# A decoder block's first MLP stage: weight sums, operand parts and m5's subtractions moved between VectorE, ScalarE and GpSimd, and the gates' buffers regrouped

## The chip, the cores and the metric

The kernel runs on one core of a Trainium2 chip. The metric is the device time of one execution in microseconds. The core's engines are TensorE (PE in the rows; its weight loads are PEld), VectorE (DVE), ScalarE (ACT), GpSimd (POOL) and SyncE (SP, which only issues DMA transfers here). Each runs its own instructions strictly in order; semaphores tie them together.

## What is computed

A hybrid decoder block on 2048 tokens of width 1024. Cut to what matters here:

```python
y_attn = dilated_attention(q, k, v)              # width 256
y_gmlp = chunked_gmlp(u, z)                      # width 512
merged = gate_a * (y_attn @ w_branch_attn) + gate_b * (y_gmlp @ w_branch_gmlp)
x = x + rmsnorm(merged @ w_out)
h = rmsnorm(x)
a = relu(h @ w_mlp_in)                           # 1024 -> 4096: first MLP stage
x = x + rmsnorm((a * a) @ w_mlp_out)             # second MLP stage
```

`gate_a` and `gate_b` are sigmoids of columns of the block's first projection; they wait in DRAM (`gated`) until the merge.

## The kernel before

Every matrix product is made of three products of parts: an operand is split into a rounded high half (fp32r) and the rest, and high x high, high x low and low x high are added. A **split** is a ScalarE copy to the high half and a subtraction on VectorE or GpSimd for the low one. One product of 128 x 128 weights with 512 columns is one matmul in the rows.

**Merge** (about 1070 to 1400 us). Four chunks of 512 tokens, in the order 2, 3, 0, 1. `merge` runs over eight tiles `dt` of 128 channels. Each multiplies the attention branch (`b0`) and the gMLP branch (`b1`) on TensorE; VectorE multiplies each with its gate (L1211), adds the two (L1213), and the sum is split into `mg` (ScalarE L74, VectorE L82), from which `out_block` makes the output product `o`. A gate `g0_{c}{dt}` or `g1_{c}{dt}` is 256 KB, loaded by `load_gate` (SP L1185) into one of two pools' places and opened by ScalarE's sigmoid (L1194). A scheduler orders the instructions of this part from the order in which they are written and the places that are free. Between the gates run other transfers (`trw`, `tqw`, `spot`: sums of MLP weights and operands for the next stage).

**First MLP stage** (about 1406 to 1970 us). The 1024 x 4096 product is done as a two-level Strassen-like scheme: seven **outer products** o = 0 to 6, each with eight weight steps q (`hs_0` to `hs_55`, n = 8 o + q), each of seven small products i. That is 392 steps k, and in step k TensorE runs six matmuls or twelve in a row of two steps (L1572), into PSUM tiles `ha` (3 banks), `hb` and `hc` (3 banks together). Their results are read into the accumulators `X` (names `X`, `X_y`, `X_yt`, `X_xr`, `X_gpost`, `X_gmlp` for places in memory) or into a staging tile `e`: first reads on ScalarE (L1584) or VectorE (L1586), the others on VectorE (L1588). In this stage all engines run as written; `later(k, f, ...)` puts work behind step k.

- Weights: `hraw_n` is loaded (L1401), `combine` forms the seven parts: five sums of 256 columns on GpSimd (L1409 to L1415), and three splits `sa`, `sb`, `sc`. `staged` does such a split: ScalarE copies to the high half (L1350), copies the source once more to one of two PSUM banks (L1360), and VectorE subtracts from that (L1365).
- Operand parts: `hb` holds the raw operand of the next outer product (two at a time, `hb_o0` and `hb_o1`); its sums run on VectorE and GpSimd (`less_sub` L1469, `sum_hb` L1494). `ops_hb` splits part j into a place `spot`: if its engine is VectorE through `staged`, otherwise with one ScalarE copy (L1487) and GpSimd's subtraction (`later`'s line, L1984). At the seam of an outer product (q = 7) six parts j are split, two halves each.
- Late weight sums: `w_load`, `w_sum` and `w_store` prepare sums of `w_mlp_in` (tiles `wt`) for t = 11 to 15; `w_sum` has four operations (`which` 0 to 3), of which 0 (L1546) and 2 (L1550) are VectorE's, 1 (L1548) and 3 (L1552) GpSimd's, each waiting for the one before.
- m5: the fourth outer product's results are added to `X` and stored apart (`m5d`); after outer product 5's results have been stored they are loaded again and subtracted (`m5_sub`, L1609), four subtractions for each q, 32 in all.

Of the kernel before, what the change touches and what calls it, by code (L numbers as in the profile page):

```python
# [9 lines left out]
F32 = mybir.dt.float32  # L10
# [7 lines left out]
P = 128  # L18
# [24 lines left out]
def block_kernel(ctx, tc, a, out):  # L43
    nc = tc.nc
    pe, act, dve, pool, sp = nc.tensor, nc.scalar, nc.vector, nc.gpsimd, nc.sync
# [1005 lines left out]
    for n in range(len(units) + 1):  # L1051
        u = None
        if n < len(units):
            g, c, j = units[n]
# [85 lines left out]
    gtp = stack(e2b, "gtp", 2)  # L1140
# [39 lines left out]
    def load_gate(c, dt, wch):  # L1180
        if dt < KT and (c, dt, wch) not in gates:
            d = chunks.index(c) * KT + dt
            pl, tag = (gtp, f"gt{wch}") if c == 2 or d % (5 - 2 * wch) < 3 - wch else (gxp[0], f"gx{wch}")
            gt = pl.tile([P, 512], F32, name=f"g{wch}_{c}{dt}", tag=tag, bufs=3 - wch if pl is gtp else 2 - wch)
            sp.dma_start(gt, gate_d[wch * 8 + dt, :, c * 512:(c + 1) * 512])  # L1185
            gates[c, dt, wch] = gt

    opened, gxp, egx = set(), [], ExitStack()
# [8 lines left out]
    def merge(c, yt, between, each=None):  # L1197
        cs = slice(c * 512, (c + 1) * 512)
        mg = []
        for dt in range(KT):  # L1200
            dsl = slice(dt * P, (dt + 1) * P)
            if dt % 4 == 0:
                mg.append(mgp[dt // 4].tile([P, 2, 4, 512], F32R, name=f"mg{c}{dt}", tag="mg"))
            parts = []
            for wch, ks in ((0, range(0, 2)), (1, range(2, 6))):
                open_gate(c, dt, wch)
                gt = gates.pop((c, dt, wch))
                p = psum_mm(f"b{wch}_{c}{dt}")
                for k in ks:
                    mm3(p, wb[k][:, 0, dsl], wb[k][:, 1, dsl], yt[k][:, 0, :], yt[k][:, 1, :], k == ks[0], k == ks[-1])  # L1210
                dve.tensor_mul(gt, gt, p)  # L1211
                parts.append(gt)
            dve.tensor_add(parts[0], parts[0], parts[1])  # L1213
            split(mg[-1][:, 0, dt % 4, :], mg[-1][:, 1, dt % 4, :], parts[0])
            if c != 2:
                load_gate(c, dt + 5, 0)
                load_gate(c, dt + 3, 1)
            elif not dt:
                w = bot.tile([P, D], F32, name="gates3", tag="xr")
                for n, key in enumerate(((c, 5, 1), (c, 6, 0))):  # L1220
                    gates[key] = w[:, n * 512:(n + 1) * 512]
                    sp.dma_start(gates[key], gate_d[key[2] * 8 + key[1], :, c * 512:(c + 1) * 512])
            elif dt > 2:
                load_gate(c, dt + 3, 1)
                load_gate(c, dt + 4, 0)
            if dt < KT - 1:
                for wch in range(2):
                    open_gate(c, dt + 1, wch)
            if each:
                each(dt)  # L1230
            if dt in between:
                between[dt]()
        return mg
# [88 lines left out]
    W_EARLY = 11  # L1322
# [47 lines left out]
    NQ, HQ = NF // 2, NF // 4  # L1370
# [137 lines left out]
    def later(k, f, *args):  # L1508
        todo.setdefault(k, []).append((f, args))
# [32 lines left out]

    def w_sum(t, which):
        a11, a12, a21, a22 = outer_t["w", t]
        if which == 0:
            dve.tensor_add(a22, a21, a22)  # L1546
        elif which == 1:
            pool.tensor_sub(a21, a11, a21)  # L1548
        elif which == 2:
            dve.tensor_sub(a11, a22, a11)  # L1550
        else:
            pool.tensor_sub(a12, a12, a11)  # L1552

# [45 lines left out]
    m5_ = {}  # L1599
# [6 lines left out]
    def m5_sub(q, f):  # L1606
        for c in range(2):
            x_ = X[2 * q + f][:, c * 512:(c + 1) * 512]
            pool.tensor_sub(x_, x_, m5_.pop((q, f, c)))  # L1609

    def hstep(k, n, i):

# [21 lines left out]
                    later(k + ((7, 11, 16) if o + 1 in LESS else (3, 8, 16))[m] + w, sum_hb, key(o + 1, w), part, eng)  # L1634
        if q == HQ - 1 and USE[i][0] < 6:
            j = USE[i][0] + 1
            ops_hb(k, o + 1, j, (None if j == 1 else dve, dve if o in (0, 3) else pool))
            if j == 1:
                for w in range(2):
                    later(k + 3 + w, sum_hb, key(o + 1, w), "T4", (dve, pool)[w])  # L1640
# [31 lines left out]
    for n, c in enumerate(chunks):  # L1672
        if n:
            mg = merge(c, yt, {0: flush, 2: flush}, lambda dt: merge_pieces(c, dt))
        for i in range(4):
# [2 lines left out]
            last.append(b)  # L1678
            if n < 3 and not i:
                yt = load_y(chunks[n + 1])  # L1680
                for dt, wch in ((0, 0), (0, 1), (1, 0), (1, 1), (2, 0), (2, 1), (3, 0), (4, 0)):
                    with behind():
                        load_gate(chunks[n + 1], dt, wch)
            if n < 3:
# [262 lines left out]
        for f, d, args in ((outer_load, 0, ()), (outer_sum, 4, (0,)), (outer_sum, 6, (2,)), (outer_store, 9, ())):  # L1947
            later(t + d, f, n, *args)
    for n in range(NF // 2 - W_EARLY):
        t = (37, 43, 48, 124, 127)[n]  # L1950
        for f, d, args in ((w_load, 0, ()), (w_sum, 4, (0,)), (w_sum, 4, (1,)), (w_sum, 5, (2,)), (w_sum, 6, (3,)),
                           (w_store, 7, ())):
            later(t + d, f, W_EARLY + n, *args)
    for q in range(HQ):
        t = 7 * (5 * HQ + 4) + 19 * q // 2
        for f in range(2):
            later(t + 5 * f, m5_load, q, f)
            later(t + 5 * f + 5, m5_sub, q, f)
    gfin = None
    for k, (_, stage, n, i) in enumerate(yorder):  # L1960
        if not stage:
# [125 lines left out]
```

## Time and profile before

| what | value |
|---|---|
| time, median of 3 runs | 2595.82 us (2593.57 to 2597.63) |
| time of the profiled execution | 2597.95 us |
| its span, first to last instruction | 2596.2 us |
| mean granted clock of TensorE | 0.993 |
| TensorE / VectorE / ScalarE / GpSimd busy | 98% / 65% / 49% / 53% |

The rows further down are in microseconds from the start of the span. In a timeline a line has the start, the duration, the engine, the source line, the operation with its output and inputs, and in brackets the idle time of the engine just before, with what ended it. SPq is SyncE's queue. In a row of windows the granted clock of TensorE stands behind POOL: 1.00 is 2.4 GHz, 0.50 is 1.2 GHz.

### The profile page before, as it was taken

What the parts mean: (1) busy time and instruction counts of PE and PEld (TensorE: products, weight loads), DVE (VectorE), ACT (ScalarE), POOL (GpSimd) and SP (SyncE); (2) the same over time, 40 slices, a digit from 0 to 9 for tenths busy, and PEclk for the clock granted to TensorE, in tenths of its full rate; (3) what the DMA queues carried; (4) which work ended last, traced back from release to release, by engine and by line L of the source; (5) the groups of instructions that cost most, each with busy time, mean ns of one, the idle gap of its engine ahead of it and who ended that gap; (6) DMA issues with size and microseconds to landing.
All of it is one profiled execution on the core that took longest, in us unless ns stands there. A gap on an engine that the chain in (4) does not pass through costs nothing. (4 is left out here: it accounts for less than half of the span.)

```text
span 2596.2 us, 36297 instructions
## 1 busy us (share of the span) xinstructions
PE 2550.3 (98%) x12122; PEld 2126.4 (82%) x12122; DVE 1687.8 (65%) x3071; ACT 1282.7 (49%) x2702; POOL 1367.1 (53%) x1377
## 2 busy tenths in 40 slices
PE   9999999999999999999999999999999999999998
PEld 8888888888888887787787777878878888888886
DVE  5676565444443446776676678778877676666767
ACT  5213211244445434554435745675447676666755
POOL 0363254275545554311113757777798667777634
PEclk9999999999999999999999999999999999999999
DMA  8779778989897899877766766457884222122236
GB/s 319 281 248 327 256 233 277 316 251 287 269 325 228 228 291 327 283 253 249 266 235 234 244 202 211 139 175 214 265 269 146 84 95 72 67 90 90 90 114 211
DMA packets 413294, 568.73 MB, mean 219 GB/s; under 512 B 58930, under 2 KB 247602, under 8 KB 412083
## 3 DMA queue, kind: packets, MB, share of 16 engines
q1 hardware_dynamic: 387600, 504.73, 59.7%
q0 software_dynamic: 15616, 55.06, 5.5%
q10 hardware_dynamic: 9890, 6.62, 0.8%
q8 instruction: 96, 1.57, 0.2%
q14 instruction: 92, 0.75, 0.1%
HBM read 362.16 MB, written 204.14 MB: 218 GB/s over the span
## 5 line engine op out<-in xcount | busy, mean ns | idle before, releaser
L1572 PE MATMUL ha<-spot,hs 128*128 128x512 f32 x1344 | 327.9, 392 | 12.9 <-DVE e L1586 3.6
L1882 PE MATMUL ya<-spot,s 128*128 128x512 f32 x1344 | 324.0, 389 | 0.8 <-DVE X_yt L1890 0.5
L1572 PEld LDWEIGHTS ha<-spot,hs 128*128 128x128 f32 x1344 | 252.1, 188 | 69.9 <-DVE e L1586 5.2
L1882 PEld LDWEIGHTS ya<-spot,s 128*128 128x128 f32 x1344 | 252.0, 188 | 54.2 <-DVE X_yt L1890 0.9
L1350 ACT ACTIVATE s<-sraw 128x512 fp32r<-128x512 f32 x168 | 105.3, 627 | 152.5 <-POOL sraw L1411 113.3
L1350 ACT ACTIVATE hs<-hraw 128x512 fp32r<-128x512 f32 x168 | 105.1, 626 | 140.6 <-POOL hraw L1411 110.0
L1572 PE MATMUL hc<-spot,hs 128*128 128x512 f32 x672 | 173.4, 394 | 0.8 <-DVE X_y L1588 0.8
L731 PE MATMUL g<-opA,spots 128*128 128x512 f32 x672 | 171.4, 399 | 2.1 <-DVE cv L763 2.1
L1882 PE MATMUL yc<-spot,s 128*128 128x512 f32 x672 | 170.5, 389 | 0.0
L731 PE MATMUL g<-opB,spots 128*128 128x512 f32 x648 | 164.0, 397 | 0.0
L1572 PEld LDWEIGHTS hc<-spot,hs 128*128 128x128 f32 x672 | 128.2, 191 | 28.3 <-DVE X_y L1588 1.2
L99 PE MATMUL x<-hT_a,wq 128*128 128x512 f32 x384 | 149.7, 390 | 0.0
L100 PE MATMUL x<-hT_a,wq 128*128 128x512 f32 x384 | 149.4, 389 | 0.0
L101 PE MATMUL x<-hT_a,wq 128*128 128x512 f32 x384 | 149.4, 389 | 0.0
L1882 PEld LDWEIGHTS yc<-spot,s 128*128 128x128 f32 x672 | 126.1, 188 | 26.2
L74 ACT ACTIVATE hl<-r 128x512 fp32r<-128x512 f32 x48 | 30.4, 633 | 236.8 <-POOL r L332 89.0
L731 PEld LDWEIGHTS g<-opA,spots 128*128 128x128 f32 x672 | 121.5, 189 | 24.3 <-issue 2.5
L82 POOL TENSOR_TENSOR spots<-gr,spots 128x512 fp32r<-128x512 f32 x98 | 128.5, 1315 | 23.8 <-DMA gr<-in_w_in_dram 8.7
L1743 ACT ACTIVATE sraw<-sraw 128x1024 f32<-128x1024 f32 x128 | 134.7, 1052 | 1.7
L731 PEld LDWEIGHTS g<-opB,spots 128*128 128x128 f32 x648 | 116.9, 188 | 21.2
L82 POOL TENSOR_TENSOR spot<-w2r,spot 128x512 fp32r<-128x512 f32 x79 | 101.0, 1305 | 50.2 <-ACT spot L74 50.2
L76 POOL TENSOR_SCALAR spots<-gr 128x512 fp32r<-128x512 f32 x86 | 55.4, 644 | 130.6 <-PE g L731 92.6
(466 smaller groups left out, 6758.1 us busy)
## 6 DMA issues: line engine op xcount, KB each, us to landing
sraw<-sd SPq DMA_DIRECT2D x128, 256.0 KB, 3.3
qk<-hl SPq DMA_DIRECT2D x24, 1024.0 KB, 5.7
qq<-qk SPq DMA_DIRECT2D x96, 256.0 KB, 5.3
sd<-e SPq DMA_DIRECT2D x64, 256.0 KB, 4.6
hraw<-wsd SPq DMA_DIRECT2D x32, 512.0 KB, 4.7
w2r<-in_w_mlp_out_dram SPq DMA_DIRECT2D x16, 1024.0 KB, 9.0
g<-gated SPq DMA_DIRECT2D x56, 256.0 KB, 5.4
gr<-sgd SPq DMA_DIRECT2D x53, 256.0 KB, 4.9
```

What stands on the lines that cost most here:

```text
L74: act.activation(hi, src, AF.Copy)
L76: pool.tensor_scalar(hi, src, 1.0, 1.0, op0=OP.mult, op1=OP.mult)
L82: (pool if lo_eng == "pool" else dve).tensor_sub(lo, src, f32(hi))
L99: pe.matmul(ps, lh, rh, start=start, stop=False)
L100: pe.matmul(ps, lh, rl, start=False, stop=False)
L101: pe.matmul(ps, ll, rh, start=False, stop=stop)
L731: pe.matmul(p, w[:, l, k], h[:, r, k], start=i in (1, 6, 5, 4) and not k and not m, stop=k == 3 and m == 2, skip_group_check=True)
L1350: act.activation(hi, src, AF.Copy)
L1572: pe.matmul(p, w[:, l, S_AT[i], kk * P:(kk + 1) * P], b[r], start=i in (1, 2, 5) and not kk and not z, stop=kk == 1 and z == 2, skip_group ...
L1743: act.activation(sraw_[n], sraw_[n], func)
L1882: pe.matmul(p, s[:, l], w[r], start=i in (1, 2, 5) and not m and not o, stop=m == 1 and o == 2, skip_group_check=True)
```

## The change

Four things are changed.

1. `load_gate` spreads the gates over four places for each kind (before: five for `g0`, three for `g1`), and after tile `dt` loads both gates of `dt` + 4 (before: `g0` of `dt` + 5 and `g1` of `dt` + 3). Ahead of a chunk `g1` of tile 3 is loaded instead of `g0` of tile 4.
2. For t = 13, 14 and 15 all four operations of `w_sum` are GpSimd's. The loads of t = 14 and 15 go from steps 124 and 127 to 122 and 134, the sums and stores with them.
3. At the seams behind outer products 0 and 3, the second half of the parts j = 2, 4 and 6 is GpSimd's instead of VectorE's, which also drops the second ScalarE copy.
4. m5's loads and subtractions get other steps. The subtractions ran from step 313 on, every 9 or 10 steps for q (f = 1 five steps behind f = 0). Now they run at step 7 (40 + q) + 24 for q up to 3 (304 to 325) and + 38 from q = 4 on (346 to 367), f = 1 three steps behind f = 0, loads five steps ahead. For q over 3 the first of two subtractions is VectorE's (8 operations).

```diff
--- before.py
+++ after.py
@@ -1180,8 +1180,8 @@
     def load_gate(c, dt, wch):
         if dt < KT and (c, dt, wch) not in gates:
             d = chunks.index(c) * KT + dt
-            pl, tag = (gtp, f"gt{wch}") if c == 2 or d % (5 - 2 * wch) < 3 - wch else (gxp[0], f"gx{wch}")
-            gt = pl.tile([P, 512], F32, name=f"g{wch}_{c}{dt}", tag=tag, bufs=3 - wch if pl is gtp else 2 - wch)
+            pl, tag = (gtp, f"gt{wch}") if c == 2 or d % 4 < 3 - wch else (gxp[0], f"gx{wch}")
+            gt = pl.tile([P, 512], F32, name=f"g{wch}_{c}{dt}", tag=tag, bufs=3 - wch if pl is gtp else 1 + wch)
             sp.dma_start(gt, gate_d[wch * 8 + dt, :, c * 512:(c + 1) * 512])
             gates[c, dt, wch] = gt
 
@@ -1213,8 +1213,8 @@
             dve.tensor_add(parts[0], parts[0], parts[1])
             split(mg[-1][:, 0, dt % 4, :], mg[-1][:, 1, dt % 4, :], parts[0])
             if c != 2:
-                load_gate(c, dt + 5, 0)
-                load_gate(c, dt + 3, 1)
+                load_gate(c, dt + 4, 0)
+                load_gate(c, dt + 4, 1)
             elif not dt:
                 w = bot.tile([P, D], F32, name="gates3", tag="xr")
                 for n, key in enumerate(((c, 5, 1), (c, 6, 0))):
@@ -1542,12 +1542,13 @@
 
     def w_sum(t, which):
         a11, a12, a21, a22 = outer_t["w", t]
+        e = dve if t < W_EARLY + 2 else pool
         if which == 0:
-            dve.tensor_add(a22, a21, a22)
+            e.tensor_add(a22, a21, a22)
         elif which == 1:
             pool.tensor_sub(a21, a11, a21)
         elif which == 2:
-            dve.tensor_sub(a11, a22, a11)
+            e.tensor_sub(a11, a22, a11)
         else:
             pool.tensor_sub(a12, a12, a11)
 
@@ -1606,7 +1607,7 @@
     def m5_sub(q, f):
         for c in range(2):
             x_ = X[2 * q + f][:, c * 512:(c + 1) * 512]
-            pool.tensor_sub(x_, x_, m5_.pop((q, f, c)))
+            (dve if q > 3 and not c else pool).tensor_sub(x_, x_, m5_.pop((q, f, c)))
 
     def hstep(k, n, i):
 
@@ -1634,7 +1635,7 @@
                     later(k + ((7, 11, 16) if o + 1 in LESS else (3, 8, 16))[m] + w, sum_hb, key(o + 1, w), part, eng)
         if q == HQ - 1 and USE[i][0] < 6:
             j = USE[i][0] + 1
-            ops_hb(k, o + 1, j, (None if j == 1 else dve, dve if o in (0, 3) else pool))
+            ops_hb(k, o + 1, j, (None if j == 1 else dve, dve if o in (0, 3) and j % 2 else pool))
             if j == 1:
                 for w in range(2):
                     later(k + 3 + w, sum_hb, key(o + 1, w), "T4", (dve, pool)[w])
@@ -1678,7 +1679,7 @@
             last.append(b)
             if n < 3 and not i:
                 yt = load_y(chunks[n + 1])
-                for dt, wch in ((0, 0), (0, 1), (1, 0), (1, 1), (2, 0), (2, 1), (3, 0), (4, 0)):
+                for dt, wch in ((0, 0), (0, 1), (1, 0), (1, 1), (2, 0), (2, 1), (3, 0), (3, 1)):
                     with behind():
                         load_gate(chunks[n + 1], dt, wch)
             if n < 3:
@@ -1947,15 +1948,15 @@
         for f, d, args in ((outer_load, 0, ()), (outer_sum, 4, (0,)), (outer_sum, 6, (2,)), (outer_store, 9, ())):
             later(t + d, f, n, *args)
     for n in range(NF // 2 - W_EARLY):
-        t = (37, 43, 48, 124, 127)[n]
+        t = (37, 43, 48, 122, 134)[n]
         for f, d, args in ((w_load, 0, ()), (w_sum, 4, (0,)), (w_sum, 4, (1,)), (w_sum, 5, (2,)), (w_sum, 6, (3,)),
                            (w_store, 7, ())):
             later(t + d, f, W_EARLY + n, *args)
     for q in range(HQ):
-        t = 7 * (5 * HQ + 4) + 19 * q // 2
+        t = 7 * (5 * HQ + q) + (24 if q < 4 else 38)
         for f in range(2):
-            later(t + 5 * f, m5_load, q, f)
-            later(t + 5 * f + 5, m5_sub, q, f)
+            later(t + 3 * f - 5, m5_load, q, f)
+            later(t + 3 * f, m5_sub, q, f)
     gfin = None
     for k, (_, stage, n, i) in enumerate(yorder):
         if not stage:
```

From L1546 on a line of the new kernel has a number that is one higher. The first place is GpSimd's order in outer product 5, from the last sum of `hs_46` to the first of `hs_47`; `m5_...` are m5's tiles, `hb_61` the operand for outer product 6. Before:

```order
L1415 TENSOR_TENSOR hraw_46_16986<-hraw_46_16986 128x256
L1609 TENSOR_TENSOR X_yt4_13018<-X_yt4_13018,m5_000_17060 128x512
L1609 TENSOR_TENSOR X_yt4_13018<-X_yt4_13018,m5_001_17062 128x512
L1494 TENSOR_TENSOR hb_61_16810<-hb_61_16810 128x512
L1984 TENSOR_TENSOR spot0_12747<-hb_61_16810,spot0_12747 128x512
L1609 TENSOR_TENSOR X_yt5_13019<-X_yt5_13019,m5_010_17129 128x512
L1609 TENSOR_TENSOR X_yt5_13019<-X_yt5_13019,m5_011_17131 128x512
L1494 TENSOR_TENSOR hb_61_16810<-hb_61_16810 128x512
L1409 TENSOR_TENSOR hs_47_17193<-hraw_47_17075,hs_47_17193 128x256
```

and now:

```order
L1415 TENSOR_TENSOR hraw_46_16982<-hraw_46_16982 128x256
L1494 TENSOR_TENSOR hb_61_16798<-hb_61_16798 128x512
L1985 TENSOR_TENSOR spot0_12747<-hb_61_16798,spot0_12747 128x512
L1610 TENSOR_TENSOR X_yt1_13021<-X_yt1_13021,m5_110_17074 128x512
L1610 TENSOR_TENSOR X_yt1_13021<-X_yt1_13021,m5_111_17076 128x512
L1610 TENSOR_TENSOR X_yt2_13022<-X_yt2_13022,m5_200_17133 128x512
L1610 TENSOR_TENSOR X_yt2_13022<-X_yt2_13022,m5_201_17135 128x512
L1494 TENSOR_TENSOR hb_61_16798<-hb_61_16798 128x512
L1409 TENSOR_TENSOR hs_47_17199<-hraw_47_17079,hs_47_17199 128x256
```

The four subtractions in these rows are now those of `m5_110` to `m5_201`; the six of `m5_000` to `m5_101` stand ahead of `hs_46`.

The second place is VectorE's order in outer product 2, from a read of `hc_17` into `X_yt` to the read of `sb` for `hs_20`; `wt14x` and `wt15x` are tiles of the late weight sums. Before:

```order
L1588 TENSOR_TENSOR X_yt0_13020<-X_yt0_13020,hc_17_14705 128x512
L1546 TENSOR_TENSOR wt143_14716<-wt142_14715,wt143_14716 128x512
L1588 TENSOR_TENSOR X_0_13024<-X_0_13024,ha_19_14774 128x512
L1550 TENSOR_TENSOR wt140_14713<-wt143_14716,wt140_14713 128x512
L1588 TENSOR_TENSOR X_yt3_13023<-X_yt3_13023,ha_18_14676 128x512
L1365 TENSOR_TENSOR hs_20_14783<-sa_20_14786,hs_20_14783 128x512
L1588 TENSOR_TENSOR X_yt3_13023<-X_yt3_13023,hc_18_14802 128x512
L1546 TENSOR_TENSOR wt153_14754<-wt152_14753,wt153_14754 128x512
L1469 TENSOR_TENSOR hb_30_14573<-hb_30_14573 128x512
L1588 TENSOR_TENSOR X_0_13024<-X_0_13024,hb_19_14823 128x512
L1550 TENSOR_TENSOR wt150_14751<-wt153_14754,wt150_14751 128x512
L1365 TENSOR_TENSOR hs_20_14783<-sb_20_14821,hs_20_14783 128x512
```

and now:

```order
L1589 TENSOR_TENSOR X_yt0_13020<-X_yt0_13020,hc_17_14707 128x512
L1589 TENSOR_TENSOR X_0_13024<-X_0_13024,ha_19_14762 128x512
L1589 TENSOR_TENSOR X_yt3_13023<-X_yt3_13023,ha_18_14670 128x512
L1365 TENSOR_TENSOR hs_20_14774<-sa_20_14777,hs_20_14774 128x512
L1589 TENSOR_TENSOR X_yt3_13023<-X_yt3_13023,hc_18_14792 128x512
L1469 TENSOR_TENSOR hb_30_14567<-hb_30_14567 128x512
L1589 TENSOR_TENSOR X_0_13024<-X_0_13024,hb_19_14807 128x512
L1365 TENSOR_TENSOR hs_20_14774<-sb_20_14805,hs_20_14774 128x512
```

The four sums on `wt` tiles are gone; the reads of `ha`, `hb` and `hc` stand next to one another.

The third place is ScalarE's order in the merge of chunk 3: sigmoids of gates (L1194) and copies for the merged tile (`mg`, L74). Before:

```order
L1194 ACTIVATE g1_34_10931<-g1_34_10931 128x512
L74 ACTIVATE mg30_10856<-g0_32_10542 128x512
L1194 ACTIVATE g0_36_10929<-g0_36_10929 128x512
L1194 ACTIVATE g1_35_10966<-g1_35_10966 128x512
L74 ACTIVATE mg30_10856<-g0_33_10546 128x512
L1194 ACTIVATE g0_37_10964<-g0_37_10964 128x512
L1194 ACTIVATE g1_36_11009<-g1_36_11009 128x512
L74 ACTIVATE mg34_11019<-g0_34_10548 128x512
```

and now:

```order
L1194 ACTIVATE g1_35_10931<-g1_35_10931 128x512
L74 ACTIVATE mg30_10856<-g0_32_10542 128x512
L1194 ACTIVATE g0_35_10929<-g0_35_10929 128x512
L1194 ACTIVATE g1_36_10966<-g1_36_10966 128x512
L74 ACTIVATE mg30_10856<-g0_33_10546 128x512
L1194 ACTIVATE g0_36_10964<-g0_36_10964 128x512
L1194 ACTIVATE g1_37_11011<-g1_37_11011 128x512
L1194 ACTIVATE g0_37_11009<-g0_37_11009 128x512
L74 ACTIVATE mg34_11021<-g0_34_10884 128x512
```

`g0_35` and `g1_36` now have the places of `g0_36` and `g1_35`, and the sigmoid of `g0_37` stands ahead of the copy for `g0_34`.

## Rows read from the trace of the kernel before

**Rows 1.** The page's first part: engine, busy us (share of the span), instructions.

```profile
PE 2550.3 (98%) x12122; PEld 2126.4 (82%) x12122; DVE 1687.8 (65%) x3071; ACT 1282.7 (49%) x2702; POOL 1367.1 (53%) x1377
```

**Rows 2.** TensorE's waits, 1100 to 2000 us: us in total, times, longest.

```profile
PE b L99 <- DVE g L1211: 4.9, 3, 1.8
PE ha L1572 <- DVE e L1586: 3.6, 3, 2.2
PE ha L1572 <- DVE X_yt L1588: 2.5, 1, 2.5
PE ha L1572 <- DVE X L1588: 2.3, 1, 2.3
PE ha L1572 <- ACT X_y L1584: 1.5, 1, 1.5
PE ha L1572 <- ACT e L1584: 1.4, 1, 1.4
PE hc L1572 <- DVE X_y L1588: 0.8, 1, 0.8
```

**Rows 3.** Windows: us, busy us of PE, PEld, DVE, ACT, POOL; clock, DMA share, GB/s.

```profile
1267.10:1270.50 3.40, 3.40 (x9) 2.65 (x8) 3.37 (x7) 0.73 (x2) 0.72 (x1) 0.50 0.95 287
1499.20:1502.60 3.40, 3.40 (x9) 2.65 (x8) 3.16 (x6) 2.24 (x5) 1.94 (x3) 0.50 0.63 136
1608.40:1611.80 3.40, 3.40 (x10) 2.66 (x9) 3.40 (x5) 0.00 (x0) 3.24 (x4) 0.50 0.97 323
1891.70:1895.10 3.40, 3.40 (x8) 2.69 (x9) 3.40 (x6) 2.48 (x6) 3.40 (x4) 0.50 0.70 216
```

**Rows 4.** Timeline of ScalarE, chunk 3's merge: start, duration, [idle before <-releaser].

```profile
1179.67 0.63 ACT L1194 ACTIVATE g<-g 128x512 f32<-128x512 f32 x1 [4.34 <-DMA g<-gated]
```

**Rows 5.** Timelines of ScalarE and SyncE's queue at the end of chunk 1.

```profile
1357.14 0.63 ACT L74 ACTIVATE mg<-g 128x512 fp32r<-128x512 f32 x1 [2.08 <-DVE g L1213]
1355.42 0.33 SPq L1310 DMA_DIRECT2D tqw<-in_w_mlp_in_dram  x1
```

**Rows 6.** Timelines of ScalarE, VectorE and GpSimd, 1480 to 1501 us.

```profile
1485.48 0.60 ACT L1360 ACTIVATE sw<-hb 128x512 f32<-128x512 f32 x1 [0.26 <-DVE spot L1365]
1482.26 0.69 DVE L1550 TENSOR_TENSOR wt<-wt,wt 128x512 f32<-128x512 f32 x1 [0.70 <-POOL wt L1548]
1491.05 1.21 DVE L1550 TENSOR_TENSOR wt<-wt,wt 128x512 f32<-128x512 f32 x1 [0.81 <-POOL wt L1548]
1489.72 1.30 POOL L1548 TENSOR_TENSOR wt<-wt,wt 128x512 f32<-128x512 f32 x1 [3.72 <-DVE wt L1546]
1500.51 0.74 POOL L1409 TENSOR_TENSOR hs<-hraw,hs 128x256 fp32r<-128x256 f32 x1 [3.96 <-ACT hs L1407]
```

**Rows 7.** Timelines of VectorE and GpSimd, 1604 to 1607 us.

```profile
1604.10 1.75 DVE L1550 TENSOR_TENSOR wt<-wt,wt 128x512 f32<-128x512 f32 x1 [1.29 <-POOL wt L1548]
1606.38 0.67 DVE L1588 TENSOR_TENSOR X<-X,ha 128x512 f32<-128x512 f32 x1
1604.03 1.28 POOL L1469 TENSOR_TENSOR hb<-hb 128x512 f32<-128x512 f32 x1
```

**Rows 8.** Windows, the 20 us around outer product 4's first steps.

```profile
1720.00:1740.00 20.00, 17.26 (x74) 13.31 (x73) 16.91 (x29) 19.39 (x38) 13.54 (x14) 1.00 0.31 94
```

**Rows 9.** Windows at 1880 us; timelines of GpSimd, VectorE and ScalarE before it.

```profile
1880.00:1900.00 20.00, 17.52 (x71) 14.02 (x70) 12.21 (x21) 10.49 (x21) 19.37 (x20) 0.91 0.75 235
1841.36 1.30 POOL L1469 TENSOR_TENSOR hb<-hb 128x512 f32<-128x512 f32 x1 [4.85 <-DMA hb<-tqd]
1854.60 2.55 POOL L1609 TENSOR_TENSOR X_yt<-X_yt,m 128x512 f32<-128x512 f32 x2
1867.38 0.69 DVE L1365 TENSOR_TENSOR hs<-sb,hs 128x512 fp32r<-128x512 f32 x1 [1.99 <-ACT sb L1360]
1889.69 0.69 DVE L1365 TENSOR_TENSOR hs<-sb,hs 128x512 fp32r<-128x512 f32 x1 [5.15 <-ACT sb L1360]
1888.53 0.63 ACT L1350 ACTIVATE hs<-hraw 128x512 fp32r<-128x512 f32 x1 [4.31 <-POOL hraw L1411]
```

## The prediction

> **What bounds the kernel now.** I read the page's engine shares first, then TensorE's waits between 1100 and 2000 us (the merge and the first MLP stage, which hold everything that the diff touches), then its granted clock behind the gaps, then the timeline of each engine around them. TensorE is busy for 2550.3 of 2596.2 us [rows 1]: what can be won is a handful of short gaps, and no engine's average matters. The waits name them [rows 2]: three in the merge behind VectorE's gate product (4.9 us together), and in the first MLP stage 2.2 and 0.8 us at the seam of outer products 0 and 1 (and 1.5 behind ScalarE's `X_y`), 2.3 us in product 2, about 2.8 at the seam of 3 and 4 (ScalarE's 1.4, and the 1.4 that is left of VectorE's 3.6 without the 2.2), and 2.5 us in product 5. I call the last four A, B, C and D. Behind the longest of them, and behind one of the gates', the granted clock is 0.50 for 3.4 us (1.2 instead of 2.4 GHz) [rows 3], and 3.4 x 0.5 = 1.7 us of work is lost with it; behind the gaps of 1.5 us and less it is not. So 4.9 + 1.7 (gates), 2.2 + 0.8 + 1.7 (A without its 1.5), 2.3 + 1.7 (B), 2.8 (C) and 2.5 + 1.7 (D) are at stake, 22.3 us in all.
>
> **Gates: 0, from -6.6 to +1.** VectorE's gate product stands in its order behind the split of an earlier merged tile (`mg`), whose first half is ScalarE's; and ScalarE waits 4.34 us for a gate's transfer ahead of it [rows 4]. With the new places the second kind of gate is loaded for one tile step further ahead. But it goes out when it did: the place that `g1_35` took before, and `g1_36` takes now, comes free by a VectorE read of the same tile step, so the transfer leaves at the same instant and only its name is later. ScalarE's order shows the sigmoid of that transfer still in front of the split of `g0_33`: `g0_36, g1_35, split` became `g0_35, g1_36, split`. TensorE's next gate is there sooner, but the strict order keeps everything behind the one that lands last. So 0.
>
> At the end of chunk 1 the loads of two operands change places: `spot51` goes first, `spot41` behind one more 512 KB transfer, about where `tqw` went out at 1355.42 [rows 5]; and ScalarE and VectorE now split both ahead of the merged tile of `g0_16`, which ScalarE split at 1357.14 [rows 5]. If the load takes 3 to 4 us, `spot41` lands near 1359 and the tile comes 2 us later or somewhat more; TensorE's output products have about as much begun. It costs 0 to 2 us; I take **+0.9**.
>
> **A: -3.6, from -5 to 0.** Of the late weight sums, the piece t = 13 takes two operations off VectorE; of the operand parts, three second halves take three ScalarE copies (0.60 us [rows 6]) and three VectorE subtractions away. Five operations of 1.30 us, 6.5 us in all, come to GpSimd, which stands idle there for 3.72 and 3.96 us [rows 6], the first time waiting for one of VectorE's two sums. That has room. VectorE's wait of 0.81 us for GpSimd's `wt` at 1491.05, and its 1.21 us sum behind it [rows 6], stand right ahead of the `X_y` read that ends the 0.8 us gap: both leave VectorE, and the gap goes. The read that ends the 2.2 us gap lies further down the same order; with one copy and one subtraction less in front of it I leave it half, 1.1, and the half clock goes with the other half, as none followed 1.5. The gap of 1.5 stays: VectorE still runs t = 12's sum, waits 0.70 us for GpSimd there [rows 6], and now runs it ahead of the `sb` read for which ScalarE wants its bank. 0.8 + 1.1 + 1.7 = 3.6.
>
> One row speaks against taking VectorE's sums to GpSimd: VectorE's `wt` sum at 1604.10 took 1.75 us while GpSimd ran an operation until 1605.31 [rows 7], against 0.69 undisturbed [rows 6], so VectorE lost 1.06 of the 1.21 us that were left of GpSimd's. The Trainium skill ("SBUF — State Buffer", section "SBUF: two separate sides") has a rule for it: a VectorE instruction with two SBUF inputs and a GpSimd instruction that reads SBUF need the same port pair, and the second blocks until the first is done. By that rule, with which the row agrees, each moved sum could hold up a VectorE sum that stays, and with one of these near the 2.2 us gap A would be -2.3 and not -3.6.
>
> **B: -4.0, from -4 to 0.** TensorE waits 2.3 us for the `X` read of VectorE at 1606.38; ahead of it VectorE waits 1.29 us for GpSimd's `wt` and then takes 1.75 [rows 7]. These 3.0 us leave VectorE with the sums of t = 14 and 15, so gap and half clock, 2.3 + 1.7, go. What may take the place: t = 15 is loaded seven steps later, and its four sums, all GpSimd's now (5.2 us, where they were 2.6), stand ahead of the weight sums of `hs_22`, and its stores ahead of the load of `hraw_23`. No row shows what slack these have; 0 to 2 us may come back 15 to 25 us later, and all 4 at worst.
>
> **C: -1.0, from -2.8 to 0.** ScalarE is busy for 19.4 of 20 us around C [rows 8], so its copies are the bound. Three of them, 0.60 us each, go over 16 us: one ahead of the first gap, the others ahead of the second, half a microsecond at each.
>
> **m5's subtractions, and D: +4.8, from -4.2 to +9.4.** Eight of 32 go to VectorE in outer product 6, at 0.7 us each, where TensorE has no gaps: 0 if their loads, five steps ahead, arrive in time. The other thing is where the first sixteen lie: from step 304 on and before the seam, instead of from 313 and through it. GpSimd's order has 6 subtractions ahead of `hs_46`'s sums where there was none, 10 instead of 4 ahead of `hs_47`, 14 instead of 6 ahead of `hs_48`, 16 instead of 10 ahead of `hs_49`. Six of them take 6 x 2.55 / 2 = 7.7 us [rows 9]. GpSimd can't begin earlier: it stands at a transfer of `hb` until 1841.36 [rows 9], which precedes the first subtraction in the new order too, and around the seam it has 19.4 of 20 us to do [rows 9]. D is a GpSimd gap already: TensorE waits for an `X` read of VectorE's that stands behind 5.15 us of waiting for ScalarE's `sb` of `hs_49`, and ScalarE behind 4.31 us of waiting for GpSimd's sums [rows 9]. The steps from 329 to 346 are kept free, but of the pairs ahead of `hs_49` only two lay in them, and those now come earlier still. A walk down the new order with undisturbed durations puts `hs_49`'s sums 6.0 us later than they were. TensorE, which has lost 2.5 us by then, will have lost 8.5, part of it earlier: 1.4 at `hs_46`, about 3.5 at `hs_47`, where VectorE already waits 1.99 us for such a read without a gap [rows 9]. That is +6.0 with one half clock behind the last gap, as now, and +4.3 if this gap has become short; I take 4.8. With the full 7.7 and a second half clock it is 9.4.
>
> **Sum.** 0 + 0.9 - 3.6 - 4.0 - 1.0 + 4.8 = **-2.9 us**. Against the profiled execution's own 2597.95 that gives 2595.05; it lay 2.1 us over the median of the runs (2595.82), on which it gives 2592.9. I say **2593.0**; with A and B down to -2, and D between 2 and 7, its own range is 2589 to 2599.
>
> **Rivals.** (1) D clears. The subtractions are done early, ScalarE's and VectorE's waits at `hs_46` and `hs_47` swallow the lateness, and GpSimd is free for `hs_49`: D is -4.2 instead of +4.8, the time 2593.0 - 9.0 = 2584.0. For it: product 5 has one gap only, and the subtractions beside it move away. Against it: the order, in which GpSimd finds no idle time to catch up in. Chance 0.20. (2) The gates' lead is real, because the transfer that lands last is not the one I name: -6.6 and no +0.9, 2593.0 - 7.5 = 2585.5. For it: places are what holds the loads back. Against it: ScalarE's order. 0.12. (3) GpSimd becomes the first stage's bound, and the kernel slower. What VectorE loses comes back as late `hs` sums at A, B and C as at D, from the point where the moved work exceeds GpSimd's idle time there (6.5 us against 7.7 at A; none is left at D). Then A, B and C give 0, D +6.0 and chunk 1 +0.9: 2595.8 + 6.9 = 2602.7. For it: D's row, where it is so already. Against it: the idle time at A. 0.16. (4) The forecast, 0.50. The 0.02 left are for (1) and (2) together, 2576.5.
>
> **How the numbers follow.** A measurement of this kernel can tell about 0.2%, 5.2 us, from no change: faster is below 2590.6, slower above 2601.0. Faster is (1), (2), both, and 0.04 of the forecast: 0.38. Slower is (3) and 0.01 of the forecast: 0.17. The rest is 0.45. The range, 2583 to 2603, takes in the centres of all cases but the last; the outer halves of (1) and (3) and the joint case lie outside, about 0.2.
>
> **What would show it.** Gates: three gaps of 1.4 to 1.8 us behind VectorE's gate product as before; none would be rival 2. A: one gap of 1.5 us, none of 0.8, one near 1.1, and full clock. B: none, or a short one near `hs_22`. C: two gaps of 0.7 to 0.9. D: gaps near steps 319, 326 and 340, with VectorE waiting for `sb`; none would be rival 1, and more of the kind at A and B rival 3. The prediction fails most surely if GpSimd begins the subtractions before 1841 us, or if gaps appear past 1900 us, where VectorE takes eight of them.

## The result and the profile after

The changed kernel takes 2601.14 us (median of 20 runs, 2594.65 to 2606.91), the kernel before 2596.61 (20 runs, 2590.34 to 2602.08). The ratio is 1.0016 with a 95% interval of 1.0009 to 1.0023: by it 4.2 us slower, between 2.3 and 6.0 (the two medians lie 4.5 apart). The forecast had said 2.9 us faster. The time lies inside the wide range (2583 to 2603) and within 0.2% of before, but the sign was wrong, and the likeliest case's own range (2589 to 2599) misses it. Further down, the ratio for the weight sums alone leaves out one execution that took 5195.24 us, twice the ten others.

The two profiled executions hide this: 2597.95 us before, 2598.09 after. They are single executions out of a spread of 12 us. What can be compared in them is stretches between the same products on TensorE. These are the starts of the first product behind the merge's first transposes, of the first MLP stage's first step, of the steps behind A's last and C's last gap, and of the second stage. Before (start, duration, operation, [idle before <-releaser]):

```profile
1069.62 0.79 PE L100 MATMUL b<-yt,wb 128*128 128x512 f32 x1 [2.54 <-DVE yt L82]
1406.12 0.73 PE L1572 MATMUL ha<-spot,hs 128*128 128x512 f32 x2 [0.78 <-ACT junk L1259]
1498.15 1.25 PE L1572 MATMUL ha<-spot,hs 128*128 128x512 f32 x4 [2.22 <-DVE e L1586]
1736.52 0.73 PE L1572 MATMUL ha<-spot,hs 128*128 128x512 f32 x2 [1.19 <-DVE e L1586]
1970.17 1.20 PE L1882 MATMUL ya<-spot,s 128*128 128x512 f32 x4 [0.49 <-DVE X_yt L1890]
```

After:

```profile
1066.51 0.50 PE L100 MATMUL b<-yt,wb 128*128 128x512 f32 x1 [2.54 <-DVE yt L82]
1402.19 0.74 PE L1573 MATMUL ha<-spot,hs 128*128 128x512 f32 x2 [0.78 <-ACT junk L1259]
1495.23 1.00 PE L1573 MATMUL ha<-spot,hs 128*128 128x512 f32 x2 [2.17 <-DVE e L1587]
1729.10 1.20 PE L1573 MATMUL ha<-spot,hs 128*128 128x512 f32 x4 [0.22 <-DVE e L1587]
1970.21 0.96 PE L1883 MATMUL ya<-spot,s 128*128 128x512 f32 x3 [0.33 <-DVE X_yt L1891]
```

| stretch | before | after | difference |
|---|---|---|---|
| ahead of the merge (nothing is changed there) | 1069.62 | 1066.51 | -3.1 |
| merge, with the gates | 336.50 | 335.68 | -0.8 |
| first MLP stage to A's last gap | 92.03 | 93.04 | +1.0 |
| on to C's last gap (with B) | 238.37 | 233.87 | -4.5 |
| on to the second stage (with D) | 233.65 | 241.11 | +7.5 |

Without the first row, an accident of two executions, the rest costs 3.2 us, not far from the 4.2 of the ratio. The rows are no exact prices, since half clock behind gaps that the change doesn't touch is in them too. At the start of the first MLP stage (the wait for `tt`) the gap was 1.38 us before, with full clock behind it; now it is 1.91 with half clock (first window below), which makes about 2.2 us of the third row. In the merge the clock fell three times before and once now.

What the gaps say is that B and C give about what was promised, D takes more than was reckoned, and A gives little. TensorE's waits from 1100 to 2000 us after the change (the lines that bear on [rows 2]; us in total, times, longest):

```profile
PE b L99 <- DVE g L1211: 5.7, 3, 3.2
PE ha L1573 <- DVE X L1589: 4.1, 3, 2.4
PE ha L1573 <- DVE e L1587: 3.1, 3, 2.2
PE hb L1573 <- ACT tt L1275: 1.9, 1, 1.9
PE ha L1573 <- DVE X_gpost L1589: 1.8, 1, 1.8
PE ha L1573 <- ACT X_y L1585: 1.5, 1, 1.5
PE ha L1573 <- DVE X_yt L1589: 1.2, 1, 1.2
PE ha L1573 <- ACT e L1585: 0.9, 1, 0.9
PE ha L1573 <- DVE X_y L1589: 0.3, 1, 0.3
```

A's 0.8 us behind `X_y` is gone; B's 2.3 us has become 0.26 (part of the 4.1); C's are 0.85, 0.71 and 0.22. The 2.2 us at A stays, and reads of `X`, `X_gpost`, `X_y` and `X_yt` now hold TensorE five times in outer product 5: 1.40, 2.40, 1.82, 0.33 and 1.19 us. These are the first three:

```profile
1845.05 1.67 PE L1573 MATMUL ha<-spot,hs 128*128 128x512 f32 x6 [1.40 <-DVE X L1589]
1857.54 2.93 PE L1573 MATMUL ha<-spot,hs 128*128 128x512 f32 x6 [2.40 <-DVE X L1589]
1870.65 2.66 PE L1573 MATMUL ha<-spot,hs 128*128 128x512 f32 x6 [1.82 <-DVE X_gpost L1589]
```

In the first MLP stage the granted clock (behind POOL, as in [rows 3]) fell behind the gap for `tt`, behind A's 2.2 us gap as before, and twice at D:

```profile
1410.20:1413.60 3.40, 3.40 (x9) 2.65 (x8) 3.40 (x6) 2.76 (x6) 1.89 (x3) 0.50 1.01 383
1495.50:1498.90 3.40, 3.40 (x9) 2.63 (x9) 2.99 (x6) 2.27 (x5) 2.48 (x4) 0.50 1.05 308
1857.30:1860.70 3.40, 3.16 (x8) 2.48 (x9) 3.08 (x5) 1.82 (x4) 3.40 (x4) 0.50 0.45 125
1871.00:1874.40 3.40, 3.40 (x10) 2.62 (x9) 3.40 (x6) 2.28 (x5) 3.40 (x3) 0.50 0.65 190
```

### The profile page after: what moved, and what is told of

Same layout as the page of the kernel before. It is cut to its first block, busy times and chain, and to the rows that moved or that the text cites. A ratio compares the mean times of both kernels' runs of the same rounds, so it can differ in the third digit from the quotient of the medians.

```text
span 2596.3 us, 36299 instructions
## 1 busy us (share of the span) xinstructions
PE 2547.3 (98%) x12122; PEld 2122.9 (82%) x12122; DVE 1687.4 (65%) x3067; ACT 1279.9 (49%) x2696; POOL 1374.3 (53%) x1381
## 5 line engine op out<-in xcount | busy, mean ns | idle before, releaser
L74 ACT ACTIVATE hl<-r 128x512 fp32r<-128x512 f32 x48 | 30.4, 633 | 236.6 <-POOL r L332 89.0
```

The source lines that it names most:

```text
L74: act.activation(hi, src, AF.Copy)
```

## Experiments

Two theories stood against each other at first. **Theory**: GpSimd's strict order ahead of the seam of products 5 and 6 makes D's loss, and the other parts gain. **Rival**: the loss is from the gates or the weight sums. Times are medians of 5 to 12 executions; ratios, and the differences given from them, are to the kernel before run on the same chip.

**m5 alone.** The kernel before with only this:

```diff
-            pool.tensor_sub(x_, x_, m5_.pop((q, f, c)))
+            (dve if q > 3 and not c else pool).tensor_sub(x_, x_, m5_.pop((q, f, c)))
...
-        t = 7 * (5 * HQ + 4) + 19 * q // 2
+        t = 7 * (5 * HQ + q) + (24 if q < 4 else 38)
...
-            later(t + 5 * f, m5_load, q, f)
-            later(t + 5 * f + 5, m5_sub, q, f)
+            later(t + 3 * f - 5, m5_load, q, f)
+            later(t + 3 * f, m5_sub, q, f)
```

> The kernel before with m5's loads and subtractions as in the change, nothing else. Theory (GpSimd's order at the seam of products 5 and 6 costs it): several gaps in outer product 5 that sum to 6 to 8 us with one or two stretches of half clock, where before has one of 2.5 with one; the time 6 to 8 us over before (ratio about 1.0027). Rival (the loss is from elsewhere, the gates or the weight sums): one gap of 2 to 3 us there, the time within 2 us of before.

Measured: 2604.86 us, ratio 1.0033 (1.0021 to 1.0044), 8.6 us slower, somewhat more than the 6 to 8 expected. TensorE's waits from 1820 to 1930 us are now these, where before has 2.5 us in all:

```profile
PE ha L1572 <- DVE X_gpost L1588: 3.3, 1, 3.3
PE ha L1572 <- DVE X L1588: 3.0, 2, 2.4
PE ha L1572 <- DVE X_yt L1588: 0.5, 1, 0.5
PE hc L1572 <- DVE X L1588: 0.3, 1, 0.3
```

That is 7.0 us, with 6.8 us of half clock behind the longest. So m5's part alone costs more than the whole change does.

**m5 as before.** The changed kernel with that part undone:

```diff
-            (dve if q > 3 and not c else pool).tensor_sub(x_, x_, m5_.pop((q, f, c)))
+            pool.tensor_sub(x_, x_, m5_.pop((q, f, c)))
...
-        t = 7 * (5 * HQ + q) + (24 if q < 4 else 38)
+        t = 7 * (5 * HQ + 4) + 19 * q // 2
...
-            later(t + 3 * f - 5, m5_load, q, f)
-            later(t + 3 * f, m5_sub, q, f)
+            later(t + 5 * f, m5_load, q, f)
+            later(t + 5 * f + 5, m5_sub, q, f)
```

> The changed kernel with m5's loads and subtractions as before. Theory: the one gap of 2.5 us in outer product 5 is back and the others there are gone; the time is 7 us under the changed kernel, 3 to 4 us under before (ratio about 0.9988). Rival: within 2 us of the changed kernel.

Measured: 2591.21 us, ratio 0.9982 (0.9973 to 0.9990), 4.7 us under before; one gap of 2.48 us in product 5. The rest of the change is worth something, and m5's part overturns it. The rival falls.

**m5 halved, at the new steps.** Is it GpSimd's count of operations, or the steps themselves?

```diff
-            (dve if q > 3 and not c else pool).tensor_sub(x_, x_, m5_.pop((q, f, c)))
+            (pool if c else dve).tensor_sub(x_, x_, m5_.pop((q, f, c)))
```

> The changed kernel with the first of each two m5 subtractions on VectorE for all q instead of q over 3 only: ahead of the weight sums of hs_49 GpSimd then has 8 subtractions, where the changed kernel has 16 and before 10. Theory (GpSimd's lateness alone makes the gaps): no gap over 1 us in outer product 5, the time 7 to 11 us under the changed kernel, 3 to 6 us under before. Rival (VectorE, or the loads that come earlier, would be the bound): gaps of some 5 us in outer product 5 remain behind VectorE, the time within 3 us of the changed kernel.

Measured: 2592.11 us, ratio 0.9986 (0.9977 to 0.9994), 3.6 under before. Four gaps remain (0.8, 0.3, 1.3 and 1.2 us), so "none over 1 us" missed, but no half clock follows them. Taking eight operations off GpSimd gave back 7.8 us, so VectorE's taking them cost less than that.

**m5 halved, at the old steps.** The kernel before with the weight sums and operand parts of the change, and with that same line, at m5's old steps.

> The kernel before with the changes to the weight sums and to the operand parts, the gates as before, m5 at its steps of before, but the first of each two subtractions on VectorE for all q: ahead of hs_49 GpSimd has 5 of them instead of 10. Theory (GpSimd's order makes D): no gap over 1 us and no half clock in outer product 5, the time 8 to 10 us under before (ratio about 0.9965), the fastest so far. Rival (D is VectorE's, or the transfers' of m5): a gap of 2 us or more stays there, the time 3 to 5 us under before.

Measured: 2589.93 us, ratio 0.9970 (0.9958 to 0.9981), 7.8 under before, just short of the 8 to 10 expected. In product 5 a single wait is left (TensorE, 1820 to 1930 us):

```profile
PE ha L1573 <- DVE X_yt L1589: 0.4, 1, 0.4
```

In GpSimd's order 10 subtractions stand ahead of `hs_49`'s sums in the kernel before, 5 in this one and 16 in the changed one. With 5 the 2.5 us at D shrink to 0.4, with 16 they become 7. So D belongs to GpSimd, in the kernel before as well. The number alone isn't the measure: the 8 at the new steps left 3.6 us of gaps, more than the 10 at the old ones, so it matters too which tile's sums they stand ahead of.

**Gates.** Once undone from the changed kernel, once alone on the kernel before (the cuts below are of the second):

```diff
-            pl, tag = (gtp, f"gt{wch}") if c == 2 or d % (5 - 2 * wch) < 3 - wch else (gxp[0], f"gx{wch}")
+            pl, tag = (gtp, f"gt{wch}") if c == 2 or d % 4 < 3 - wch else (gxp[0], f"gx{wch}")
...
-                load_gate(c, dt + 5, 0)
-                load_gate(c, dt + 3, 1)
+                load_gate(c, dt + 4, 0)
+                load_gate(c, dt + 4, 1)
...
```

> The changed kernel with the gates' places and loads as before. Theory (the four places bring nothing, and cost a little at the end of chunk 1): three gaps behind the gate product, none of 0.6 us at the output product of chunk 1; the time 0 to 3 us under the changed kernel. Rival (the four places do help): 2 us or more over the changed kernel.

> The kernel before with the gates' places and loads as in the change, nothing else. Theory (the split behind the transfer that lands last still holds VectorE): three gaps behind the gate product of 5 to 7 us together and one of about 0.6 at chunk 1's output product; the time 0 to 3 us over before. Rival (four places help): gaps under 3 us together, the time 3 to 6 us under before.

Measured: undone 2596.57 us, ratio 1.0005 (0.9994 to 1.0017), which can't be told from the changed kernel's 1.0016; alone 2597.34 us, ratio 1.0000 (0.9991 to 1.0009). Within 2.3 us the places neither help nor cost. The gaps behind the gate product differ from one profile to the next with the places the same: 2.2 to 6.5 us together in the eight with the old places, 5.2 to 6.8 in the five with the new ones, in one to three gaps, so "three gaps" held in neither of these two kernels and one profile says little of them. What does go with the new places is the gap at chunk 1's output product: 0.5 to 1.2 us in all five profiles with them, and none in the eight with the old ones.

**Weight sums alone.**

```diff
+        e = dve if t < W_EARLY + 2 else pool
         if which == 0:
-            dve.tensor_add(a22, a21, a22)
+            e.tensor_add(a22, a21, a22)
...
-            dve.tensor_sub(a11, a22, a11)
+            e.tensor_sub(a11, a22, a11)
...
-        t = (37, 43, 48, 124, 127)[n]
+        t = (37, 43, 48, 122, 134)[n]
```

> The kernel before with the late weight sums as in the change, nothing else. The gap of product 2 (2.3 us) goes, with its half clock, and 0 to 1 us comes back some 10 us later; at the seam of products 0 and 1 the 0.8 us gap goes and the 2.2 us one stays, if the place that a staging tile takes over from the weight sums is what holds it; the time 3 to 5 us under before (ratio about 0.9985). Rival (GpSimd is the bound there too): other gaps come in their stead, the time within 1.5 us of before.

Measured: 2592.31 us, ratio 0.9982 (0.9972 to 0.9991), 4.7 under before. At A the 0.8 us gap is gone, the other, which was expected to stay, shrank to 1.74, and no half clock follows. But in this execution B's gap came back, 2.6 us long, at another place:

```profile
1607.14 1.40 DVE L1469 TENSOR_TENSOR hb<-hb 128x512 f32<-128x512 f32 x1 [4.66 <-DMA hb<-h2d]
1609.80 0.80 PE L1573 MATMUL ha<-spot,hs 128*128 128x512 f32 x1 [2.60 <-DVE X L1589]
```

VectorE waits for an operand's transfer. On SyncE's queue the four loads of t = 15 (1 MB) stand now right ahead of it. In the eight kernels with that order VectorE waits 1.5 to 4.7 us for `hb` in this stretch, with the old order 0.5 to 1.4. That the loads ahead of it make the wait longer is argued from the order and these waits; no run shows it by itself. In three of the eight the gap lies at this place and goes with the wait: 2.4 and 0.5 us (m5 as before), 2.9 and 1.0 (gates undone), 4.7 and 2.6 here.

In three others it lies seven steps later and has another cause: 0.26 us in the changed kernel, 0.7 with m5 halved at the old steps, 0.95 in the kernel with the earlier sum below. There GpSimd's four sums of t = 15 stand ahead of those for `hs_22`, ScalarE waits for these and VectorE for ScalarE (in the changed kernel, ahead of the gap at 1621.14):

```profile
1618.64 0.63 ACT L1350 ACTIVATE hs<-hraw 128x512 fp32r<-128x512 f32 x1 [6.44 <-POOL hraw L1411]
1619.80 0.69 DVE L1365 TENSOR_TENSOR hs<-sb,hs 128x512 fp32r<-128x512 f32 x1 [2.28 <-ACT sb L1360]
```

**Operand parts alone.**

```diff
-            ops_hb(k, o + 1, j, (None if j == 1 else dve, dve if o in (0, 3) else pool))
+            ops_hb(k, o + 1, j, (None if j == 1 else dve, dve if o in (0, 3) and j % 2 else pool))
```

> The kernel before with the operand parts shared as in the change, nothing else. Theory: at the seam of products 3 and 4 the gaps go from 2.8 to 1.9 us; at the seam of 0 and 1 the 0.8 us gap stays, since VectorE's weight sum is in its place, and the 2.2 us one shrinks by 0.5 or stays; the time 0 to 2 us under before (ratio about 0.9996), so that the four parts of the change add up to what they do together within 3 us. Rival (GpSimd's three subtractions at each seam hold up the hs sums): new gaps there, the time 1 us or more over before.

Measured: 2592.76 us, ratio 0.9983 (0.9974 to 0.9992), 4.4 under before: more than expected. C goes from 2.7 to 1.8 us (1.38, 0.17 and 1.19 before; 0.85, 0.73 and 0.22); at A the 2.2 us gap shrinks to 1.18, with full clock behind it (the 0.8 one grows to 1.39). Alone, the weight sums give 4.7 and the operand parts 4.4; with m5's +8.6 and the gates' 0 that makes -0.5, against +4.2 measured for all. The errors of each (about 2.5) could hold that, but A shows part of it: either part alone shortens the gap ahead of the read (to 1.74 and 1.18), and with either alone the read waits for nothing; both together leave it at 2.15 to 2.18, in the changed kernel and in the four variants with both (m5 as before, gates undone, m5 halved at either steps).

**The last sum for t = 13 one step earlier.** Why does A's 2.2 us stay when both are done? These are VectorE's read that ends the gap, before (it waits for nothing) and in the changed kernel, and there GpSimd's operation ahead of it:

```profile
1497.41 0.68 DVE L1586 TENSOR_TENSOR e<-X_yt,ha 128x512 f32<-128x512 f32 x1
1494.49 0.69 DVE L1587 TENSOR_TENSOR e<-X_yt,ha 128x512 f32<-128x512 f32 x1 [0.81 <-POOL wt L1553]
1493.19 1.26 POOL L1553 TENSOR_TENSOR wt<-wt,wt 128x512 f32<-128x512 f32 x1
```

The read writes the staging tile `e801`, which shares its four places with the weight tiles (`rx`, tag `c1`), and takes over one that GpSimd's last sum of t = 13 still reads. GpSimd now runs an operand part's subtraction and both new sums ahead of that one. The experiment puts this sum directly behind the third, on top of the changed kernel:

```diff
-        for f, d, args in ((w_load, 0, ()), (w_sum, 4, (0,)), (w_sum, 4, (1,)), (w_sum, 5, (2,)), (w_sum, 6, (3,)),
+        for f, d, args in ((w_load, 0, ()), (w_sum, 4, (0,)), (w_sum, 4, (1,)), (w_sum, 5, (2,)), (w_sum, 5 if n == 2 else 6, (3,)),
```

> The changed kernel with the last of the four sums for t = 13 one step earlier, so that GpSimd runs it directly behind the third and ahead of two sums for hs_9. Theory (the read e that ends the 2.2 us gap at the seam of products 0 and 1 waits for that sum, because its staging tile takes over a place of the weight tiles): the read waits for nothing of GpSimd's any more and the gap shrinks by about 0.8 to 1.4 us, and no half clock follows. Rival (VectorE's queue ahead of the read sets it): the gap stays within 0.3 us of 2.2.

Measured (one execution, whose time decides nothing): 2599.15 us. The wait is 0.15 us, the gap 1.50 instead of 2.17, just short of the 0.8 less that was expected, and the clock stays full behind it:

```profile
1495.05 0.69 DVE L1587 TENSOR_TENSOR e<-X_yt,ha 128x512 f32<-128x512 f32 x1 [0.15 <-POOL hraw L1414]
1495.80 0.50 PE L1573 MATMUL ha<-spot,hs 128*128 128x512 f32 x1 [1.50 <-DVE e L1587]
```

**All of it together.** m5 halved at its old steps, with this earlier sum:

> The kernel before with the changes to weight sums and operand parts, m5 halved between the engines at its old steps, and the last sum for t = 13 one step earlier. Theory (each of the two waits named costs by itself): at the seam of products 0 and 1 a gap of 1.5 us and one of 1.5 to 1.8 with no half clock, none over 1 us in product 5; the time 9 to 11 us under before (ratio about 0.996), 2 us under the same kernel without the earlier sum. Rival (what is saved at one seam is given back behind it): the time within 1 us of that kernel, 7 to 8 under before.

Measured: 2584.27 us, ratio 0.9954 (0.9942 to 0.9967), 11.9 us under before and the fastest kernel here. At A the gap ahead of the read `e` is 1.53 us, as expected; the other, behind ScalarE's `X_y`, is 2.12 where 1.5 was expected, and 0.4 is left at D, with full clock behind all of them. The time lies past the expected 9 to 11 us, within the interval. What the earlier sum adds to m5 halved (11.9 against 7.8) isn't clear of noise, since the intervals overlap. Part of it may be the clock's: in this profile no half clock lies between 1080 and 1970 us, where the twelve others have two to five such stretches.

**t = 15 loaded five steps earlier.** On top of that, to take B's remainder:

```diff
-        t = (37, 43, 48, 122, 134)[n]
+        t = (37, 43, 48, 122, 129)[n]
```

> The kernel of m5_halved_last with t = 15 loaded at step 129 instead of 134, five steps farther ahead of the last pair of hb loads of outer product 2 to 3. Theory (the 1 MB of t = 15 on SyncE's queue directly ahead of that pair makes VectorE wait 1.7 to 4.7 us at an hb subtraction, from which B's remainder of 0.3 to 2.6 us comes): VectorE's wait for hb there is under 1 us, no gap over 0.3 us between 1590 and 1630 us, the time 0 to 2 us under m5_halved_last. Rival (GpSimd's sums of t = 15 ahead of hs_22 make the remainder): a gap of 0.5 to 2 us stays or moves up, the time equal or higher.

Measured: 2593.87 us, ratio 0.9985 (0.9976 to 0.9994), 8.0 us slower than without it by the ratios (9.6 by the medians). The theory of the queue falls, since VectorE's wait for `hb` grew to 3.0 us. The rival is right about the sums, though the gap is longer than it said: GpSimd waits for t = 15's transfer, runs its four sums ahead of `hs_21`'s, and TensorE stands for 1.1 and then 4.0 us.

```profile
1604.69 1.29 POOL L1547 TENSOR_TENSOR wt<-wt,wt 128x512 f32<-128x512 f32 x1 [4.29 <-DMA wt<-in_w_mlp_in_dram]
1615.59 0.69 DVE L1365 TENSOR_TENSOR hs<-sb,hs 128x512 fp32r<-128x512 f32 x1 [4.64 <-ACT sb L1360]
1616.93 1.13 PE L1573 MATMUL ha<-spot,hs 128*128 128x512 f32 x3 [3.98 <-DVE X L1589]
```

So of the two steps tried 134 is the better one: it is late enough for the sums to stand behind `hs_21`.

## Why the prediction was wrong, step by step

- **Gates, 0**: right. Alone they measure 0.0 us (within 2.3). The profile agrees with the mechanism: in chunk 3's merge ScalarE still waits for a gate's transfer ahead of the split, 4.34 us in [rows 4] and 3.75 here

```profile
1177.61 0.63 ACT L1194 ACTIVATE g<-g 128x512 f32<-128x512 f32 x1 [3.75 <-DMA g<-gated]
```

- **Chunk 1's end, +0.9**: right in kind, 0.63 us. `spot41`'s split waits for its load, the tile of `g0_16` comes behind it, and TensorE waits:

```profile
1354.77 0.63 ACT L74 ACTIVATE spot<-spot 128x512 fp32r<-128x512 f32 x1 [3.66 <-DMA spot<-td]
1357.45 0.50 PE L99 MATMUL o<-wo,mg 128*128 128x512 f32 x1 [0.63 <-ACT mg L74]
```

- **B, -4.0**: near, -3.8 in the profile, where a gap of 0.26 us replaces the gap and the half clock. That remainder is at `hs_22`, as said. What was not foreseen is the other place where it can lie, VectorE's wait for a transfer of `hb`, up to 2.6 us in other kernels. Over the eight profiles with the new weight sums the gap is 0.7 us on average.
- **C, -1.0**: right, 2.7 us became 1.8, and the operand parts alone do the same.
- **A, -3.6: a step that failed.** The 0.8 us went and the 1.5 stayed, as said. But "I leave it half" had no row behind it. One copy, one subtraction and the wait were indeed taken from VectorE's queue ahead of the read, and the read came no earlier against TensorE, since a wait that had never been last took over: GpSimd's last sum on a tile whose place `e801` inherits. With gap and half clock still there A gave 0.8, 2.8 us less than the forecast; 1.7 of these are the half clock, which followed a gap of this size in some profiles and not in others (last section). The earlier sum, which takes the wait away, brought the gap to 1.50, still not the 1.1 forecast. The sum of GpSimd's idle time (7.7 us against 6.5) said that there was room, not that each result would come in time. Of the price named beside it, -2.3 by the Trainium skill's rule on the shared ports ("SBUF — State Buffer", section "SBUF: two separate sides"), this gap shows nothing: its read takes one input from SBUF and one from PSUM, and it waited for a result. Nor does the prediction show how 1.3 us less comes about; by its own numbers a gap back near 2.2 us would have cost the half clock's 1.7 as well.
- **D, +4.8: right in mechanism and sign, too small.** Measured 6.4 us by gaps and clock (7.14 + 2 x 1.7 against 2.48 + 1.7), 7.5 by the starts, 8.6 for m5 alone. GpSimd did begin the subtractions behind the transfer of `hb`, and these are its first two and, in the third row, ScalarE's copy for `hs_49`:

```profile
1836.08 1.29 POOL L1469 TENSOR_TENSOR hb<-hb 128x512 f32<-128x512 f32 x1 [6.25 <-DMA hb<-tqd]
1837.33 2.55 POOL L1610 TENSOR_TENSOR X_yt<-X_yt,m 128x512 f32<-128x512 f32 x2
1890.29 0.63 ACT L1350 ACTIVATE hs<-hraw 128x512 fp32r<-128x512 f32 x1 [1.70 <-POOL hraw L1411]
```

From the first row to the third it is 54.2 us, and 47.2 before (1841.36 and 1888.53 in [rows 9]): 7.0 later, where 6.0 had been walked. But the walk's gaps began at `hs_46`, and these two subtractions lie already ahead of `hs_45`: a gap of 1.40 us behind them was not in the sum (the transfer itself also came 2.1 us later, counted from C's last gap), and those at `hs_46` (2.40) and `hs_47` (1.82) were shared out otherwise (1.4 and 3.5). **The step that failed** is the choice of 4.8 from the walk's 6.0, on the chance that the half clock behind the last gap would go. It did go, the last gap being 1.19 us; but half clock followed the gaps at `hs_46` and `hs_47`, where the sum had one at most. The chain there, GpSimd, ScalarE and VectorE:

```profile
1859.06 5.49 POOL L1610 TENSOR_TENSOR X_yt<-X_yt,m 128x512 f32<-128x512 f32 x4
1868.15 0.63 ACT L1350 ACTIVATE hs<-hraw 128x512 fp32r<-128x512 f32 x1 [9.04 <-POOL hraw L1411]
1856.20 0.69 DVE L1365 TENSOR_TENSOR hs<-sb,hs 128x512 fp32r<-128x512 f32 x1 [3.53 <-ACT sb L1360]
1869.31 0.69 DVE L1365 TENSOR_TENSOR hs<-sb,hs 128x512 fp32r<-128x512 f32 x1 [5.19 <-ACT sb L1360]
```

VectorE's wait at `hs_47`, which was 1.99 us without a gap [rows 9], had become 5.19.

Put together: A's 2.8 us and D's 1.6 to 2.7 turn -2.9 into +1.5 to +2.6, inside the measured 2.3 to 6.0 or just below it. The rest, 1.6 to 2.7 of the 4.2 us, isn't settled; B's remainder may be a part of it, and the terms' errors are as large. Of the rivals, (3) named the engine that held up A and D; at A it was a weight sum and not an `hs` sum, and its condition, moved work against idle time, was the wrong one there, where the order of two results decided. That its 2602.7 us lies nearest to the measured 2601.14 is luck, since it denied what B and C gave. The chance given to "within 0.2%" (0.45) was the case that came true; the sign that went with it didn't.

## What to carry to other kernels

Work moved to an engine with idle time is free only if every result behind it in that engine's order still comes in time, so walk the order result by result from the first moved operation on, and count what stands ahead of each: here two operations ahead of one tile's sums (`hs_45`) came with a gap of 1.4 us, 0.6 with m5's part alone, and there was none where they weren't ahead of it. A buffer that is handed on carries the wait of its last reader along, and that wait can surface once the queue that hid it has been cleared, as at A. Several small gaps are priced better from many executions than from one profile, since a transfer's wait ahead of them, and the half clock behind them, come and go from one to the next.

## What the runs showed of the chip that was not expected

- Nearly the same gap was followed by half clock (1.2 GHz) in one profile and not in the next, so its length alone doesn't settle it. At A 2.15 to 2.22 us were followed in before, the changed kernel, the gates alone and m5 halved (both), and 2.17 to 2.19 were not in m5 as before, gates undone and m5 alone; 1.18 to 1.74 were not. At B 2.32 and 2.31 were followed in before and m5 alone, 2.32 wasn't with the gates alone and with the operand parts alone. At D 1.82 was in the changed kernel, and 2.4 wasn't in m5 alone, 13 us ahead of 3.3 that was. A fall lasted 3.4 us, the one behind m5 alone's 3.3 us twice that. The prediction had put 1.7 us down as certain where the profile of before showed one.
- VectorE's wait for the same transfer, in kernels with the same order there, went from 1.5 to 4.7 us between profiles; where the gap lay directly behind it, 2.4 to 4.7 us of wait left 0.5 to 2.6 us of gap. One profile of a kernel with such a wait isn't enough to price a gap.
